# Expert biases by a GpSimd row broadcast and VectorE adds instead of bias matmuls

## The chip, the cores and the metric

The kernel runs on one core of one Trainium2 chip. The metric is the device time of one execution in microseconds (us). The kernel before takes 2105.02 us, the median of 3 runs (2104.12 to 2105.26). A core has five engines with a queue each: TensorE (PE; PEld is its weight load), VectorE (DVE), ScalarE (ACT), GpSimd (POOL) and SyncE (SP, which here only issues DMAs). Each engine takes its instructions strictly in the order of its queue.

## The reference

One layer of a bidirectional encoder on 1024 tokens of width 1024: a hybrid mixer, cross attention to 256 memory tokens, and a mixture of experts with 32 experts of which each token takes 4. Only the last concerns us. For a block of rows `xb` of expert `e`:

```
gu   = xb @ w_gate_up[e] + b_gate_up[e]
gate = minimum(gu[:, :1024], 7);  up = clip(gu[:, 1024:], -7, 7)
glu  = gate * sigmoid(1.702 * gate)
out  = ((up + 1) * glu) @ w_down[e] + b_down[e]
```

Each `out` row is added, with its router weight, to its token's row of the result. The two bias halves of `b_gate_up[e]`, 1024 gate and 1024 up values, lie along the columns of `gu`, and each of them is the same for all rows of the block.

## The kernel before

The stages up to the router take the first 620 us or so. Then the 32 experts follow one another. Each has up to 128 rows in the main path (`main_mm`, `glu_main`, `h_main`, `y_main`: tokens on the partitions of the result) and some have 32 or 64 rows beyond these, which go by a path of their own (`rem_mm`, `h_rem`, `y_rem`); experts with such rows are called heavy, the others light, and heavy and light ones alternate for the most part.

An expert's weights are 12 chunks of 1 MB (128 partitions x 2048), loaded by SP (`load_more`, L964). Chunks 0 to 7 are gate and up, four for each half `c` of the 1024 hidden columns; chunks 8 to 11 are the down projection. Most chunks are split into a leading part and a rest (`split`, L132: ACT writes `eh`, DVE subtracts and writes `el`), and multiplied in three products, L1062 to L1064. The first 8 chunks of the first expert and the last 4 of the last are multiplied whole, L1054.

The order of all queues is written out by hand. `expert` (L1147) goes chunk by chunk; an expert has 24 places, two for each chunk, and at place p what is listed for it is issued: `glu_main` for half 0 at place 7 and for half 1 at place 15; the transposes of the hidden values (`h_main`) of half 0 at place 11 or 13 and of half 1 at 16 to 18; the transposes of the next expert's gathered rows (`x_main`, from the tile `xg`) at places 20 to 23; `y_main` (L1127), which scales the results on ACT and adds them to the tokens by a scatter DMA of POOL, after place 23. Splits run some chunks ahead of the products, by the tables `AHEAD_*`. The dictionary `agenda` holds what is put at places counted over all experts, 24 for each.

POOL has, for each expert, the gathers of the next expert's rows (L936: `xg`, and `xgr` where there are rows beyond), and the scatters L940 of `yr` and `y`. POOL also issues the first expert's later chunks.

The biases are added by matmuls: the table `BT` holds the gate biases of all experts on 64 partitions (leading parts and rests) and the up biases on the other 64, and for each expert and half two matmuls, L1049, with a one-hot column `ohr` as weights write the bias row to all rows of the banks `g` and `u` before the first product. `bias_load` and `bias_table` (L1228, L1234) make the table. `glu` (L998) then has four DVE instructions on 128 x 512: clamp of gate out of PSUM (L1000), clamp of up out of PSUM (L1002), gate times sigmoid (L1003), and (up + 1) times that (L1004), with the sigmoid on ACT (L1001). The tile tag `s4` has 7 buffers; `BT` holds one of them to the end.

Of the kernel before, what the change touches and what calls it, by code (L numbers as in the profile page):

```python
# [29 lines left out]
ALPHA = 1.702  # L30
N64 = 2
# [18 lines left out]
REM = (2, 4, 0, 4, 4, 1)  # L50
PLACE_HEAVY = (13, 17, 19, 21)
# [28 lines left out]
def kernel(ctx: ExitStack, tc: tile.TileContext, A, out, dbg=None):  # L80
# [39 lines left out]
    def rsqrt(dst, v, tmp):  # L120
        """1 / sqrt of positive columns times RS: a first guess from the exponent, three Newton steps, each without its last factor"""
# [29 lines left out]
    def sum_cols(srcs):  # L151
        """sums over the partitions, a token on each partition, 128 tokens for each column; among the products that follow"""
        b = sm_bank("colps")
        k = 0
        for src in srcs:
            for j in range(src.shape[-1] // P):
                def one(k=k, s=src[:, j * P:(j + 1) * P]):
                    nc.tensor.matmul(b[:, k:k + 1], s, ones[:, 0:1], start=True, stop=True)
                fill.append(one)
                k += 1  # L160
        return b[:, :k]

    def rms_cols(b, width, eps_scale=1.0):
        """sums of squares to 1 / rms"""
# [20 lines left out]
    def rms_row(dg, dst):  # L185
        """on every partition, a token in each column"""
# [20 lines left out]
    # weights in their order of use: raw ahead, split one ahead  # L207
# [44 lines left out]
    # ---------------------------------------------------------------- constants  # L252
# [34 lines left out]
    # ------------------------------------------------------------ x^T and the Fourier group's projection  # L287
# [75 lines left out]
    # Fourier group: fold over n <-> N - n and n <-> N/2 - n, channel transform  # L363
# [45 lines left out]
    # short convolution group  # L409
# [98 lines left out]
    # ------------------------------------------------------------ sequence transform, memory side  # L508
# [14 lines left out]
    def seq_out(ct, sb):  # L523
        """in three parts"""
# [82 lines left out]
    # ------------------------------------------------------------ output projection and first residual  # L607
# [41 lines left out]
    # ------------------------------------------------------------ attention over the memory  # L649
    # scale of the logits: rms / sqrt(head dim), one column for each token tile  # L650
# [88 lines left out]
    # v W_o for each head, then the second residual  # L739
# [20 lines left out]
    def row_table():  # L760
        """table of expert rows, all padding"""
# [17 lines left out]
    def load_bias():  # L779
        """leading parts twice, then the rests: products with leading part, rest, leading part of the weights"""  # L780
# [14 lines left out]
    # ------------------------------------------------------------ router, one tile of 128 tokens at a time  # L795
# [3 lines left out]
    BT = []  # L799

    def tile_r(x2):
        """logits of two tiles, an expert on each partition, in four parts"""
# [113 lines left out]
    # ------------------------------------------------------------ experts  # L916
# [60 lines left out]
    def whole(q):  # L977
        """chunks that are multiplied in float32 itself, where the tensor engine has the time"""
# [59 lines left out]
    def main_mm(i, j, middle=None):  # L1038
# [3 lines left out]
        if g == 0 and j >= 8:  # L1042
            s[key] = mm_bank(key)
        elif g == 0 and t == 0:
            r = s["r"]
            for t in range(2):
                tsl = slice(t * 64, t * 64 + 64)
                b = s["gu"[t] + str(c)] = mm_bank(key)
                nc.tensor.matmul(b, ohr[tsl, r:r + 1].to_broadcast([64, P]), BT[0][tsl, hs[c]], start=True, stop=False)  # L1049
        raw, wh, wl = ch[12 * i + j][:3]  # L1050
        ps = s[key]
        if wh is None:
            for k in range(4):
                nc.tensor.matmul(ps, f(l[:, 0, g * 4 + k, :]), raw[:, k, :], start=j >= 8 and g == 0 and k == 0, stop=g == 1 and k == 3)  # L1054
# [5 lines left out]
        for k in range(4):  # L1060
            kk = g * 4 + k
            nc.tensor.matmul(ps, l[:, 0, kk, :], wh[:, k, :], start=j >= 8 and g == 0 and k == 0, stop=False)  # L1062
# [7 lines left out]
    def rem_mm(i, j):  # L1070
        """rows 128.. of the pair of chunks j - 1, j: products for different rows of PSUM run side by side"""
# [18 lines left out]
    def glu_main(i, c):  # L1090
        s = st[i]
        s[f"h{c}"] = t2("hh")
        glu(s[f"h{c}"], s[f"g{c}"], s[f"u{c}"], H2, P)
# [11 lines left out]
    def h_rem(i, c):  # L1105
        """hidden values with the columns on the partitions; each sum has two parts"""
# [40 lines left out]
    def expert(i, hook=None, last=False):  # L1147
        """a chunk at a time; what else there is to do has its place after the first half of a chunk or after the chunk"""
# [50 lines left out]
    def plan(i):  # L1199
        """rows 128.. of an expert: some chunks ahead of the first 128, so that raw chunks are not held for them"""  # L1200
# [12 lines left out]
    for i in range(1, NE):  # L1213
        if rem_rows(order[i]):
            plan(i)

    # ------------------------------------------------------------ second residual, chunk by chunk
    def early():
        """positions of the static expert: rows of the first tiles within its first 128, the others beyond"""
# [7 lines left out]

    def bias_load():  # L1228
        """gate biases on the first half of the partitions, up biases on the second: a leading part and the rest of each expert"""
        BT.extend([s4("BT", [P, D], F32R), s8("braw", [P, D])])  # L1230
        for i in range(4):
            nc.scalar.dma_start(out=BT[1][i * 32:(i + 1) * 32], in_=A["b_gate_up"][:, (i // 2) * D:(i // 2 + 1) * D])

    def bias_table():  # L1234
        nc.scalar.activation(BT[0], BT[1], AF.Copy)
        for i in (32, 96):
# [369 lines left out]
```

## Time and profile before

| | |
|---|---|
| time, median of 3 | 2105.02 us (2104.12 to 2105.26) |
| span of the profiled execution | 2097.7 us |
| PE busy | 2059.9 us (98%) |
| DVE busy | 1590.7 us (76%) |
| ACT busy | 1124.9 us (54%) |
| POOL busy | 233.0 us (11%) |
| DMA moved | 514.06 MB, 245 GB/s over the span |

The span runs from the first to the last instruction of the profiled execution; the device time of a run is some 7 us longer. In a row of the timeline the first number is the start in us from the span's start, the second the busy time, then engine, line, operation, output <- input, and in brackets the idle time ahead of it with what ended it. The rows that the prediction uses stand in a section of their own below.

### The profile page before, as it was taken

Reading aid. Unit: us, or ns where it says so; the run is one execution under the profiler, and the core shown is the slowest. Engines: PE = TensorE matmul, PEld = TensorE weight load, DVE = VectorE, ACT = ScalarE, POOL = GpSimd, SP = SyncE. Lnnn points to the kernel's source line nnn. Section 1 sums busy time; section 2 is a strip of 40 time slices with the busy share of each in tenths; the row PEclk is TensorE's granted clock in tenths of the full one; section 3 lists DMA queues with packets and bytes.
Section 4 is the critical chain, followed back from the end, with each engine's and each line's share of the span. In section 5 each row is a group of like instructions: output and inputs, shape, how many; then the busy total and the mean of one; then the engine's idle time right before and its main releaser. Section 6 shows DMA issues by size and latency. Waiting matters only on the chain. (4 is left out here: it accounts for less than half of the span.)

```text
span 2097.7 us, 28863 instructions
## 1 busy us (share of the span) xinstructions
PE 2059.9 (98%) x10857; PEld 1521.2 (73%) x10857; DVE 1590.7 (76%) x2000; ACT 1124.9 (54%) x1200; POOL 233.0 (11%) x192
## 2 busy tenths in 40 slices
PE   8999999999989999999999999999999999999996
PEld 7888988888974567676777676767667767676764
DVE  6666778445666667888888897888888888888886
ACT  5233533344223455676566665667656567566764
POOL 0000100000232111011101011102111101110101
PEclk9999999999999999999999999999999999999998
DMA  4121434013266769897989887988798989798986
GB/s 156 50 65 61 146 120 157 21 41 124 94 245 252 249 224 327 296 327 267 340 309 366 300 318 272 343 304 325 278 331 313 356 296 320 273 344 306 341 303 241
DMA packets 105327, 514.06 MB, mean 245 GB/s; under 512 B 21697, under 2 KB 26050, under 8 KB 56034
## 3 DMA queue, kind: packets, MB, share of 16 engines
q1 hardware_dynamic: 83968, 445.88, 56.3%
q0 software_dynamic: 14400, 49.33, 9.6%
q10 hardware_dynamic: 6818, 16.99, 2.2%
q8 instruction: 86, 1.41, 0.3%
q14 instruction: 55, 0.45, 0.1%
HBM read 473.81 MB, written 38.34 MB: 244 GB/s over the span
## 5 line engine op out<-in xcount | busy, mean ns | idle before, releaser
L135 DVE TENSOR_TENSOR el<-raw,eh 128x2048 fp32r<-128x2048 f32 x372 | 831.3, 2287 | 134.6 <-ACT eh L134 133.1
L134 ACT ACTIVATE eh<-raw 128x2048 fp32r<-128x2048 f32 x372 | 690.5, 1908 | 7.2 <-PEq L1402 4.6
L1062 PE MATMUL g<-eh,xthl 128*128 128x512 f32 x992 | 401.3, 405 | 0.0
L1063 PE MATMUL g<-el,xthl 128*128 128x512 f32 x992 | 388.5, 392 | 2.0 <-DVE el L135 2.0
L1064 PE MATMUL g<-eh,xthl 128*128 128x512 f32 x992 | 388.2, 391 | 2.2 <-issue 2.2
L1062 PEld LDWEIGHTS g<-eh,xthl 128*128 128x128 f32 x992 | 186.5, 188 | 80.8 <-issue 42.6
L1064 PEld LDWEIGHTS g<-eh,xthl 128*128 128x128 f32 x992 | 186.6, 188 | 43.5 <-issue 2.6
L1063 PEld LDWEIGHTS g<-el,xthl 128*128 128x128 f32 x992 | 186.8, 188 | 37.9 <-DVE el L135 2.7
L1062 PE MATMUL d<-eh,hthl 128*128 128x512 f32 x496 | 205.9, 415 | 0.0
L1064 PE MATMUL d<-eh,hthl 128*128 128x512 f32 x496 | 195.0, 393 | 0.0
L1063 PE MATMUL d<-el,hthl 128*128 128x512 f32 x496 | 193.9, 391 | 0.0
L1085 PE MATMUL r<-raw,xrt 128*32 128x512 f32 (+1 forms) x1216 | 166.3, 598 | 0.7 <-ACT xrt L1036 0.7
L1001 ACT ACTIVATE sg<-g 128x512 f32<-128x512 f32 x64 | 40.4, 631 | 171.1 <-DVE g L1000 171.1
L940 POOL DMA_INDIRECT acc_d<-y,idx x31 | 78.2, 2522 | 384.7 <-ACT y L1131 302.4
L1062 PEld LDWEIGHTS d<-eh,hthl 128*128 128x128 f32 x496 | 93.2, 188 | 27.2 <-ACT xthl L134 9.2
L1064 PEld LDWEIGHTS d<-eh,hthl 128*128 128x128 f32 x496 | 93.1, 188 | 21.2
L1063 PEld LDWEIGHTS d<-el,hthl 128*128 128x128 f32 x496 | 93.6, 189 | 16.0
L1085 PEld LDWEIGHTS r<-raw,xrt 128*32 128x32 f32 (+1 forms) x1216 | 39.8, 113 | 87.0 <-issue 85.8
L134 ACT ACTIVATE hthl<-tp 128x512 fp32r<-128x512 f32 x62 | 37.1, 599 | 119.4 <-PE tp L1009 119.4
L145 PE MATMUL mm<-xh,wh 128*128 128x512 f32 x232 | 92.4, 398 | 5.8 <-ACT xh L137 5.8
L147 PE MATMUL mm<-xh,wl 128*128 128x512 f32 x232 | 91.2, 393 | 0.3 <-DVE wl L135 0.3
L146 PE MATMUL mm<-xl,wh 128*128 128x512 f32 x232 | 91.2, 393 | 0.0
(377 smaller groups left out, 3297.7 us busy)
## 6 DMA issues: line engine op xcount, KB each, us to landing
raw<-in_w_exp SPq DMA_DIRECT2D x375, 1024.0 KB
raw<-in_w_exp POOLq DMA_DIRECT2D x9, 1024.0 KB
wraw<-in_w_in SPq DMA_DIRECT2D x15, 512.0 KB
xraw<-in_xT SPq DMA_DIRECT2D x16, 256.0 KB
wraw<-in_w_k SPq DMA_DIRECT2D x8, 512.0 KB
wraw<-in_w_v SPq DMA_DIRECT2D x8, 512.0 KB
wraw<-in_w_out SPq DMA_DIRECT2D x8, 512.0 KB
xres<-in_xT SPq DMA_DIRECT2D x16, 256.0 KB
```

Of the source, the lines that this page charges most:

```text
L134: nc.scalar.activation(dh, src, AF.Copy)
L135: nc.vector.tensor_tensor(dl, src, f(dh), op=ALU.subtract)
L145: nc.tensor.matmul(ps, lh, rh, start=start and i == 0, stop=False)
L146: nc.tensor.matmul(ps, lh, rl, start=False, stop=False)
L147: nc.tensor.matmul(ps, ll, rh, start=False, stop=stop and i == n - 1)
L940: nc.gpsimd.indirect_dma_start(out=dst, out_offset=bass.IndirectOffsetOnAxis(ap=idx, axis=0), in_=src, in_offset=None, compute_op=ALU.add)
L1001: nc.scalar.activation(sg[:m, :n], g[:m, :n], AF.Sigmoid, scale=ALPHA)
L1062: nc.tensor.matmul(ps, l[:, 0, kk, :], wh[:, k, :], start=j >= 8 and g == 0 and k == 0, stop=False)
L1063: nc.tensor.matmul(ps, l[:, 0, kk, :], wl[:, k, :], start=False, stop=False)
L1064: nc.tensor.matmul(ps, l[:, 1, kk, :], wh[:, k, :], start=False, stop=g == 1 and k == 3)
L1085: nc.tensor.matmul(ps[o:o + m], lhs[:, g * 4 + kk, :], ch[12 * i + j - 1 + t][0][:, kk, :], start=k == 0 and g == 0, stop=k == 4 // n - 1 ...
```

## The change

The bias matmuls, their table and the one-hot column go. For each expert `i` and half `c`, `bias_row` loads the 512 gate and 512 up biases into partition 0 of a tile `bt` (tag `s4`, 128 x 2 x 512) by an SP DMA, and `bias_rows` has POOL add 1 to the up biases and copy partition 0 to all partitions. `BIAS` gives the places: for half 0 the load at place -3 (three places ahead of the expert's start) and the copy at place 1; for half 1 at places 5 and 9. `glu_main` adds the biases out of PSUM and takes the clamps along: 5 DVE instructions. Rows beyond 128 keep `h_rem` as it was. The comments and docstrings that the changed file leaves out are not shown.

```
+SIGMOID_LIMIT = float(1.0 / (1.0 + np.exp(-ALPHA * LIMIT)))
+BIAS = ((-3, 1), (5, 9))
...
 def main_mm(i, j, middle=None):
-        if g == 0 and j >= 8:
+        if g == 0:
             s[key] = mm_bank(key)
-        elif g == 0 and t == 0:
-            r = s["r"]
-            for t in range(2):
-                tsl = slice(t * 64, t * 64 + 64)
-                b = s["gu"[t] + str(c)] = mm_bank(key)
-                nc.tensor.matmul(b, ohr[tsl, r:r + 1].to_broadcast([64, P]), BT[0][tsl, hs[c]], start=True, stop=False)
...
 def glu_main(i, c):
-        glu(s[f"h{c}"], s[f"g{c}"], s[f"u{c}"], H2, P)
+        g, sg, u = t2("g"), t2("sg"), t2("u")
+        bt = s[f"b{c}"]
+        nc.vector.tensor_tensor(g, s[f"g{c}"], bt[:, 0, :], op=ALU.add)
+        nc.scalar.activation(sg, g, AF.Sigmoid, scale=ALPHA)
+        nc.vector.tensor_tensor(u, s[f"u{c}"], bt[:, 1, :], op=ALU.add)
+        nc.vector.tensor_scalar(u, u, LIMIT + 1.0, 1.0 - LIMIT, op0=ALU.min, op1=ALU.max)
+        nc.vector.scalar_tensor_tensor(u, sg, SIGMOID_LIMIT, u, op0=ALU.min, op1=ALU.mult)
+        nc.vector.scalar_tensor_tensor(s[f"h{c}"], g, LIMIT, u, op0=ALU.min, op1=ALU.mult)
+
+    def bias_row(i, c):
+        s = st[i]
+        bt = s[f"b{c}"] = s4("bt", [P, 2, H2])
+        nc.sync.dma_start(out=bt[0:1], in_=A["b_gate_up"][ds(s["e"], 1)].rearrange("o (t c f) -> o t c f", t=2, c=2)[:, :, c, :])
+
+    def bias_rows(i, c):
+        bt = st[i][f"b{c}"]
+        nc.gpsimd.tensor_scalar(bt[0:1, 1, :], bt[0:1, 1, :], 1.0, None, op0=ALU.add)
+        nc.gpsimd.partition_broadcast(bt.rearrange("p t f -> p (t f)"), bt[0:1].rearrange("p t f -> p (t f)"))
...
-    for i in range(1, NE):
-        if rem_rows(order[i]):
+    for i in range(NE):
+        for c, (row, rows) in enumerate(BIAS):
+            if i or c:
+                agenda.setdefault(24 * i + row, []).append(lambda i=i, c=c: bias_row(i, c))
+            agenda.setdefault(24 * i + max(rows, 0 if i else 1), []).append(lambda i=i, c=c: bias_rows(i, c))
+        if i and rem_rows(order[i]):
             plan(i)
...
-    def bias_load():
-        BT.extend([s4("BT", [P, D], F32R), s8("braw", [P, D])])
-        for i in range(4):
-            nc.scalar.dma_start(out=BT[1][i * 32:(i + 1) * 32], in_=A["b_gate_up"][:, (i // 2) * D:(i // 2 + 1) * D])
-    def bias_table():
-        nc.scalar.activation(BT[0], BT[1], AF.Copy)
-        for i in (32, 96):
-            nc.vector.tensor_tensor(BT[0][i:i + 32], BT[1][i:i + 32], f(BT[0][i:i + 32]), op=ALU.subtract)
...
-    nc.vector.tensor_copy(ohr[:, STATIC:STATIC + 1], eid[:, 4:5])
+    bias_row(0, 0)
     x_main(0, 0)
     tile_r(xD)
-    bias_table()
     x_main(0, 1)
...
-            nc.vector.tensor_copy(ohr, R)
```

POOL's queue over two experts in the middle of the program, from the scatter of one expert's results (`acc_d<-y`) to that of the one after the next, before:

```order
L940 DMA acc_d<-y,idx 1152x1024
L936 DMA xg<-h_d,idx 128x1024
L936 DMA xgr<-h_d,idr 32x1024
L940 DMA acc_d<-y,idx 1152x1024
L936 DMA xg<-h_d,idx 128x1024
L940 DMA acc_d<-yr,ids 2304x512
L940 DMA acc_d<-y,idx 1152x1024
```

And the first of these two experts now, on the same queue, with the two copies of biases into `bt`, for half 0 and half 1; an ISA row without operands names, in the built program, the library of GpSimd code that the next instruction needs (index 0 ahead of the tensor_scalar, index 1 ahead of the broadcast, which is the ISA row with operands):

```order
L941 DMA acc_d<-y,idx 1152x1024
L1106 ISA
L1106 TENSOR_SCALAR bt<-bt 1x512
L1107 ISA
L1107 ISA bt<-bt 128x1024
L937 DMA xg<-h_d,idx 128x1024
L937 DMA xgr<-h_d,idr 32x1024
L1106 ISA
L1106 TENSOR_SCALAR bt<-bt 1x512
L1107 ISA
L1107 ISA bt<-bt 128x1024
L941 DMA acc_d<-y,idx 1152x1024
```

Between two scatters stand eight more rows, four of which ask for another library, and the gathers of the next expert's rows now stand behind four of them or behind all eight.

VectorE at the end of a half of a heavy expert, `g` and `u` being the PSUM banks with the products, `hh` the hidden values, before:

```order
L135 TENSOR_TENSOR el<-raw,eh 128x2048 x6
L1000 TENSOR_SCALAR g<-g_8469 128x512
L1002 TENSOR_SCALAR u<-g_8471 128x512
L1003 TENSOR_TENSOR g<-g,sg 128x512
L1004 SCALAR_TENSOR_TENSOR hh<-u,g 128x512
L1116 TENSOR_TENSOR re<-tp,bT 128x256
```

The same place now:

```order
L137 TENSOR_TENSOR el<-raw,eh 128x2048 x6
L1090 TENSOR_TENSOR g<-g_8501,bt 128x512
L1092 TENSOR_TENSOR u<-u_8516,bt 128x512
L1093 TENSOR_SCALAR u<-u 128x512
L1094 SCALAR_TENSOR_TENSOR u<-sg,u 128x512
L1095 SCALAR_TENSOR_TENSOR hh<-g,u 128x512
L1130 TENSOR_TENSOR re<-tp,bT 128x256
```

One instruction is added, and the first of the five now reads `bt`, which POOL writes.

TensorE where one expert ends (`d`) and the next begins (`g`), before:

```order
L1064 MATMUL d_7946<-eh,hthl 128x512
L1085 MATMUL r_8034<-raw,xrt 32x512 x8
L1049 MATMUL g_8051<-BT,ohr 128x512
L1049 MATMUL g_8053<-BT,ohr 128x512
L1062 MATMUL g_8051<-eh,xthl 128x512
```

The two rows L1049 are gone from the queue at this place, and at the one in the middle of each expert; nothing else moves on TensorE.

## Rows read from the trace of the kernel before

**Rows 1.** The page's first part: engine, busy us (share), instructions.

```profile
PE 2059.9 (98%) x10857; PEld 1521.2 (73%) x10857; DVE 1590.7 (76%) x2000; ACT 1124.9 (54%) x1200; POOL 233.0 (11%) x192
```

**Rows 2.** Busy us of each engine in a stretch of experts, granted clock, DMA share, GB/s.

```profile
1200.00:1400.00 200.00, 200.00 (x1037) 141.65 (x1036) 168.30 (x149) 131.16 (x110) 26.67 (x16) 1.00 0.85 309
```

**Rows 3.** Timeline of TensorE at the start of an expert.

```profile
1043.96 0.39 PE L1063 MATMUL g<-el,xthl 128*128 128x512 f32 x1
1044.19 0.39 PE L1064 MATMUL g<-eh,xthl 128*128 128x512 f32 x1
1044.51 0.50 PE L1049 MATMUL g<-BT,ohr 64*128 64x512 f32 x2
1044.94 0.50 PE L1062 MATMUL g<-eh,xthl 128*128 128x512 f32 x1
1045.28 0.39 PE L1063 MATMUL g<-el,xthl 128*128 128x512 f32 x1
```

**Rows 4.** Groups of VectorE instructions and L1049: count, busy us, mean ns, idle before.

```profile
L1049 PE MATMUL g<-BT,ohr 64*128 64x512 f32 x128 | 32.3, 501 | 0.0
L1002 DVE TENSOR_SCALAR u<-g 128x512 f32<-128x512 f32 x64 | 44.0, 687 | 18.1 <-PE g L1064 14.3 <-PE g L1054 2.7
L1004 DVE SCALAR_TENSOR_TENSOR hh<-u,g 128x512 f32<-128x512 f32 x64 | 44.3, 692 | 2.2
L628 DVE TENSOR_TENSOR mm<-mm,row 128x512 f32<-128x512 f32 x32 | 22.3, 698 | 15.2 <-PE mm L147 15.0
L696 DVE TENSOR_SCALAR pr<-pr,st 128x256 f32<-128x256 f32 x32 | 9.9, 351 | 0.6
```

**Rows 5.** Timeline of POOL at the program's start.

```profile
0.35 0.12 POOL L1596 MEMSET const-uint8-127<- 128x1 uint8 x1
0.87 0.15 POOL L277 IOTA ioti<- 128x32 int32 x1 [0.40 <-POOLq L1596]
```

**Rows 6.** Timeline of POOL in a heavy and a light expert.

```profile
1030.96 1.45 POOL L940 DMA_INDIRECT acc_d<-yr,ids  x1 [20.16 <-ACT yr L1142]
1039.31 1.98 POOL L940 DMA_INDIRECT acc_d<-y,idx  x1 [6.89 <-DMA acc_d<-yr,ids]
1046.17 1.16 POOL L936 DMA_INDIRECT xg<-h_d,idx  x1 [4.88 <-DMA idx<-tab_d]
1047.63 0.89 POOL L936 DMA_INDIRECT xgr<-h_d,idr  x1 [0.30 <-issue]
1070.88 2.39 POOL L940 DMA_INDIRECT acc_d<-y,idx  x1 [22.37 <-ACT y L1131]
```

**Rows 7.** Timeline of SP's queue: the load of the rows' indices for that gather.

```profile
1040.13 0.34 SPq L946 DMA_DIRECT2D idx<-tab_d  x1
```

**Rows 8.** POOL by groups, and L940: ns min/median/max, first and last start us.

```profile
L198 POOL TENSOR_TENSOR row<-row,sq 128x512 f32<-128x512 f32 x6 | 10.1, 1704 | 249.2 <-ACT sq L197 249.2
L763 POOL IOTA ptab<- 128x288 int32 x1 | 0.4, 387 | 216.8 <-DVE vtl L135 216.8
L1493 POOL TENSOR_TENSOR fa<-fa,gfin 128x1024 f32<-128x1024 f32 x2 | 4.7, 2365 | 17.9 <-ACT fa L1492 17.9
L940 POOL DMA_INDIRECT acc_d<-y,idx x31: 1579/2390/3519, 700.0 to 2050.3; - x31
L940 POOL DMA_INDIRECT acc_d<-yr,ids x19 | 28.2, 1484 | 474.7 <-ACT yr L1142 377.9 <-ACT yr L1144 96.8
```

**Rows 9.** Timeline of DVE and PE around the second half's hidden values, heavy then light.

```profile
1015.32 0.68 DVE L1000 TENSOR_SCALAR g<-g 128x512 f32<-128x512 f32 x1
1017.50 0.69 DVE L1004 SCALAR_TENSOR_TENSOR hh<-u,g 128x512 f32<-128x512 f32 x1
1021.18 0.60 PE L1009 MATMUL tp<-cst,hh 128*128 128x128 f32 x4
...
1055.19 0.68 DVE L1000 TENSOR_SCALAR g<-g 128x512 f32<-128x512 f32 x1
1057.97 0.69 DVE L1004 SCALAR_TENSOR_TENSOR hh<-u,g 128x512 f32<-128x512 f32 x1
1060.53 0.60 PE L1009 MATMUL tp<-cst,hh 128*128 128x128 f32 x4
```

More of the change, by code (lines that the diff above doesn't have):

```diff
@@ L798 @@
     lt = {}
-    BT = []
     def tile_r(x2):
@@ L1053, in main_mm @@
             for k in range(4):
-                nc.tensor.matmul(ps, f(l[:, 0, g * 4 + k, :]), raw[:, k, :], start=j >= 8 and g == 0 and k == 0, stop=g == 1 and k == 3)
+                nc.tensor.matmul(ps, f(l[:, 0, g * 4 + k, :]), raw[:, k, :], start=g == 0 and k == 0, stop=g == 1 and k == 3)
                 if k % 2 and steps:
@@ L1061, in main_mm @@
             kk = g * 4 + k
-            nc.tensor.matmul(ps, l[:, 0, kk, :], wh[:, k, :], start=j >= 8 and g == 0 and k == 0, stop=False)
+            nc.tensor.matmul(ps, l[:, 0, kk, :], wh[:, k, :], start=g == 0 and k == 0, stop=False)
             nc.tensor.matmul(ps, l[:, 0, kk, :], wl[:, k, :], start=False, stop=False)
@@ L1273 @@
     xB = x2_chunk(HF, places(*two_tiles(0, xA, 0)))
-    C = two_tiles(2, xB, HF)
-    C[5].append((bias_load,))
-    xC = x2_chunk(H2, places(*C))
+    xC = x2_chunk(H2, places(*two_tiles(2, xB, HF)))
     prologue(0)
@@ L1289 @@
     dump("acc", acc_d)
-    ohr = small("ohr", [P, NE], F32R)
     ordr = small("ordr", [1, NE + 1], I32)
-    nc.vector.tensor_copy(ohr[:, STATIC:STATIC + 1], eid[:, 4:5])
+    bias_row(0, 0)
     x_main(0, 0)
     tile_r(xD)
-    bias_table()
     x_main(0, 1)
```

## The prediction

> **What bounds the kernel now.** I read the page's first part, then the busy times by stretch, then the timelines of the engines that the change touches. TensorE is busy for 98% of the span [rows 1], and in a stretch of experts for all of its 200 us, at a granted clock of 1.00 [rows 2]. So what is taken off TensorE there comes off the time, as long as nothing else becomes later than TensorE. VectorE is the next, with 168.3 of 200 us; POOL has 26.7 of 200 and mostly waits: in the timeline its scatter of `y` waits 22.37 us for ScalarE's `y` [rows 6]. POOL is nearly idle, but it stands on a loop through every expert: the gather of the next expert's rows comes behind the scatter of the last one's results, and now the biases come between.
>
> The period of that loop is read from the scatters of `y`: 31 of them, the first at 700.0 us, the last at 2050.3, so 30 periods of 45.0 us on the mean [rows 8].
>
> **What the change removes.** Each pair of bias matmuls costs more on TensorE's path than the busy time tells, since it breaks the rhythm of the products. Products start 0.23 us apart (1043.96 to 1044.19); across the pair the starts are 1044.19 and 1044.94, and the next 0.34 later [rows 3]. That is 0.75 - 0.23 + 0.34 - 0.23 = 0.63 us for each of the 64 pairs (128 matmuls, 32.3 us busy [rows 4]), 40 us in all. This is the gain if TensorE stays the bound. Making the table once, ahead of the first expert, goes too; I put that at nothing (a microsecond or two of ScalarE and VectorE in a stretch that waits for the router anyway).
>
> **What it adds on VectorE.** Four instructions become five, 64 times. Adds out of PSUM with a second input from SBUF have a row, 698 ns on the same shape; scalar_tensor_tensor has 692 [rows 4]. The clamp of `u` is from SBUF to SBUF, between 351 ns (half the width) and 687 [rows 4]; I take 0.6. So the five take 4 x 0.69 + 0.6 = 3.4 us. VectorE gains up to 64 x 0.69 = 44 us of work; in 200 us with 4.4 experts that is 8.8 x 0.69 = 6 us, 174 of 200. Not a bound. Late hidden values don't follow either: from the end of `hh` to its transposes are 3.0 us in the heavy and 1.9 us in the light expert [rows 9], more than 0.69.
>
> **What it adds on POOL.** For each half expert: a request for library 0, a tensor_scalar on 512 elements, a request for library 1, a broadcast of 1024. The two computing instructions have near rows. A two-input add of 512 elements takes 1.70 us, I take that for the tensor_scalar; an iota of 288 takes 0.387, which is 1.4 for 1024, and a two-input product of 1024 takes 2.37 [rows 8]; between them I take 1.8 for the broadcast.
>
> The price of a change of library decides this case, and the trace before shows no change of library, only one request, for the library that is already there at the program's start: from the last memset at 0.35 to the iota at 0.87 pass 0.52 us, 0.40 of them idle [rows 5]. That is the bound below. [...] The loading of one kilobyte of indices is issued at 1040.13 and its gather starts at 1046.17: 6.0 us [rows 6, 7]. And a DMA of POOL's own, the scatter of `yr` that starts at 1030.96, holds up the next scatter until 1039.31: 8.35 us [rows 6]. [...]
>
> [...]
>
> **The sum.** A half costs POOL 7.2 + 1.7 + 7.2 + 1.8 = 17.9 us, two halves 35.8, and they stand in the loop one after the other. The loop, from one scatter of `y` to the next: the scatter 2.4 (median [rows 8]); the biases of half 0, then of half 1, 35.8; the gathers that stand between or behind, 1.0 for `xg` and 0.9 for `xgr` in about 18 of 30 experts [rows 6, 8], 1.6 on the mean; VectorE's five instructions of half 1, 3.4; then the tail, from the transposes of half 1's hidden values over the last chunks and the scaling of `y` to the scatter: 1021.18 to 1039.31, 18.1 us, in the heavy expert, 1060.53 to 1070.88, 10.4 us, in the light one [rows 6, 9], with 18 heavy of 30 (19 scatters of `yr`, one of them the first expert's) 15.0. Together 2.4 + 35.8 + 1.6 + 3.4 + 15.0 = 58.2 us, against 45.0 now: TensorE no longer sets the period, and its 40 us are not gained but sit in waits. 30 x 13.2 = 396 us more. The profiled span of 2097.7 becomes about 2494, and with the 7.3 us that lie between that span and the median of 2105.02, the time is 2501, say **2500 us**.
>
> What is queued behind the waiting instructions: on VectorE, behind the add that waits for `bt`, the splits of the next chunks, and TensorE waits for these. By the tables they run some 3 to 5 chunks ahead, and a chunk lasts 45.0 / 12 = 3.75 us, so they cover 11 to 19 us of a wait once, but not one in each half expert. On POOL, behind the library requests, the gather `xg`, whose transposes stand on TensorE at places 20 to 23. On SP, the load of a `bt` row waits until a buffer of tag `s4` is free, among others until POOL has done an earlier copy, and the 1 MB chunks are queued behind it; with POOL late this comes late too, but inside the same loop. In the first expert three of its chunks and one gather stand behind a copy on POOL; that happens once, 0 to 20 us, and I leave it out of the middle value.
>
> **The rivals.**
> *Changing the library is cheap* (up to about 2 us, near the row of 0.52). Then a half is at most 2 x 2 + 3.5 = 7.5 us, the loop 15 + 22.4 = 37 us, TensorE keeps the bound, and the 40 us are gained: 2065 us. For it: the one request in the trace cost next to nothing. Against it: that one changed nothing. This is the case on the other side. Chance 0.10.
> *It breaks even*: 3 to 4 us for each change give a loop of 2.4 + 19 to 23 + 20.0 = 41 to 45 us, about the period now. 2065 to 2120 us. Chance 0.05, 0.03 of it within 0.2% of the time before (about what a measurement of this kernel can tell from no change), 0.02 slower.
> [...] From about 11 us for a change on the time is above my range. Chance 0.10.
> *VectorE becomes the bound* with its fifth instruction: by the row of 168.3 of 200 us it doesn't, and the time would then only lose part of the 40 us. Chance under 0.02, within the first rival's.
>
> **How the numbers follow.** 0.75 for the forecast, that a change of library costs between 4.5 and 11 us. Each microsecond of it is worth 4 x 30 = 120 us. 4.5 us gives a loop of 47.4 us and 2177; 11 us gives 73.4 and 2957. So the range is 2180 to 2960, which leaves out the cheap and the breaking-even cases below and the two-trip case above. Faster 0.10, same 0.03, slower 0.87.
>
> **What would show it.** The scatters of `y` should lie about 58 us apart instead of 45. POOL's timeline should show, from a tensor_scalar to its broadcast, a gap of 6 to 9 us that no engine's row explains, and the same gap ahead of the tensor_scalar. VectorE should wait for POOL at the add of `g`, about 64 times, several us each; TensorE's busy share should fall to about 82% (2020 of 2494), with its waits put down to the splits, the hidden values and `xg`. If the gap is under 2 us and TensorE stays at 98 to 100% among the experts, the price of the library was wrong and the time is near 2065. If the gaps are right and the period is not, the tail was wrong: TensorE may have done in the wait what I count behind it, as the heavy expert's tail has work for other rows in it.

## The result, and the profile after

The changed kernel takes 2666.89 us (median of 4 runs, 2658.85 to 2677.37) against 2104.57 us for the kernel before in the same comparison: a ratio of 1.2677, 95% interval 1.2642 to 1.2713. That is slower, as forecast, inside the range, and 167 us above the predicted 2500. In the following `bt` is the tile of biases, a *copy* is GpSimd's `partition_broadcast` of its first row, and a *change* is the time that GpSimd loses when it goes from one library to the other. Of the lines of the kernel after, L941 and L937 are L940 and L936 of before, L137 is L135, L1010 is L1009, and L1057 to L1059 are L1062 to L1064; `hthl` are the split, transposed hidden values, which the down products take as weights.

The page's first part, after (columns as in [rows 1]):

```profile
PE 2166.5 (81%) x10729; PEld 1594.7 (60%) x10729; DVE 1623.0 (61%) x2060; ACT 1115.6 (42%) x1199; POOL 434.9 (16%) x320
```

And the stretch from 1200 to 1400 us (columns as in [rows 2]):

```profile
1200.00:1400.00 200.00, 152.61 (x718) 106.94 (x719) 126.94 (x117) 92.24 (x78) 35.76 (x22) 0.85 0.59 211
```

No engine is near full in this stretch any more: TensorE has gone from 200.00 to 152.61 us, VectorE from 168.30 to 126.94, and POOL, the only one that has grown, is at 35.76. Nothing is slower because an engine has too much work; something waits. POOL's groups show where:

```profile
L1106 POOL TENSOR_SCALAR bt<-bt 1x512 f32<-1x512 f32 x64 | 128.4, 2006 | 566.2 <-issue 449.4 <-PE g L1059 70.8 <-DVE el L137 46.0
L1107 POOL PARTITION_BROADCAST bt<-bt x64 | 85.1, 1329 | 444.7 <-issue 391.4 <-DMA raw<-in_w_exp 37.9 <-DMA bt<-in_b_gate_up 9.5
```

The two instructions cost 213.5 us of work and 1010.9 us of idle time ahead of them, most of it put down to "issue", that is, to nothing that the profile shows: 7.9 us for each of 128. The scatters of `y` (ns min/median/max, first and last start):

```profile
L941 POOL DMA_INDIRECT acc_d<-y,idx x31: 1566/2535/3667, 716.4 to 2592.0; - x31
```

The 30 periods went from 45.0 to (2592.0 - 716.4) / 30 = 62.5 us. The first scatter is 16.4 us later than in [rows 8], and from the last one to the end of the span it is 71.8 instead of 47.4. Together 16.4 + 525 + 24.4 = 566, the difference of the spans (2663.8 and 2097.7). The loop holds 93% of the loss. Light experts lose most of it: from scatter to scatter they take 58.7 us on the mean instead of 31.7, the heavy ones 65.1 instead of 53.9 (12 and 18 periods, so 324 and 202 us).

POOL's timeline after, from a heavy expert's scatter over the whole next, light one:

```profile
1288.59 2.18 POOL L941 DMA_INDIRECT acc_d<-y,idx  x1 [7.28 <-DMA acc_d<-yr,ids]
1300.71 1.52 POOL L1106 TENSOR_SCALAR bt<-bt 1x512 f32<-1x512 f32 x1 [9.95 <-issue]
1309.28 1.30 POOL L1107 PARTITION_BROADCAST bt<-bt  x1 [7.05 <-DMA raw<-in_w_exp]
1310.78 1.19 POOL L937 DMA_INDIRECT xg<-h_d,idx  x1 [0.20 <-issue]
1312.27 0.88 POOL L937 DMA_INDIRECT xgr<-h_d,idr  x1 [0.30 <-issue]
1320.30 1.52 POOL L1106 TENSOR_SCALAR bt<-bt 1x512 f32<-1x512 f32 x1 [7.15 <-issue]
1327.71 1.30 POOL L1107 PARTITION_BROADCAST bt<-bt  x1 [5.89 <-issue]
1346.89 2.53 POOL L941 DMA_INDIRECT acc_d<-y,idx  x1 [17.87 <-ACT y L1145]
```

Four gaps of 6 to 10 us stand between short instructions, and then POOL, which has just made everybody wait, waits itself for the result of the expert that it delayed. That is the loop. (One gap is put down to a chunk's DMA: it was only the last to finish in that time.) What VectorE waits for most in the whole span (us in total, times, longest):

```profile
DVE g L1090 <- POOL bt L1107: 571.6, 62, 18.3
```

And TensorE:

```profile
PE tp L1010 <- DVE hh L1095: 349.0, 45, 18.9
PE d L1059 <- DVE hthl L137: 44.8, 17, 2.9
```

TensorE loses more than its waits. Its timeline behind one of them:

```profile
1332.47 1.09 PE L1010 MATMUL tp<-cst,hh 128*128 128x128 f32 x4 [9.33 <-DVE hh L1095]
1334.63 0.63 PE L1057 MATMUL d<-eh,hthl 128*128 128x512 f32 x1
1335.06 0.63 PE L1058 MATMUL d<-el,hthl 128*128 128x512 f32 x1
...
1344.45 0.39 PE L1058 MATMUL d<-el,hthl 128*128 128x512 f32 x1
1344.67 0.39 PE L1059 MATMUL d<-eh,hthl 128*128 128x512 f32 x1
```

Busy times and granted clock in the two pieces of it:

```profile
1332.40:1340.00 7.60, 7.53 (x26) 5.78 (x27) 6.71 (x4) 4.47 (x4) 0.00 (x0) 0.50 0.54 206
1341.50:1345.40 3.90, 3.90 (x21) 3.17 (x19) 1.39 (x2) 2.38 (x4) 0.00 (x0) 1.00 0.00 0
```

After standing for 9.33 us its products start 0.43 us apart at a granted clock of 0.50, and 0.22 us apart when the clock is back at 1.00. The same 10729 instructions are 2036.7 us of busy time in the first experiment below, which hardly waits, and 2166.5 here.

### The profile page after: what moved, and what is told of

Read it like the earlier page. It is cut to its first block, busy times and chain, and to the rows that moved or that the text cites. A ratio compares the mean times of both kernels' runs of the same rounds, so it can differ in the third digit from the quotient of the medians.

```text
span 2663.8 us, 29516 instructions
## 1 busy us (share of the span) xinstructions
PE 2166.5 (81%) x10729; PEld 1594.7 (60%) x10729; DVE 1623.0 (61%) x2060; ACT 1115.6 (42%) x1199; POOL 434.9 (16%) x320
## 3 DMA queue, kind: packets, MB, share of 16 engines
q1 hardware_dynamic: 84224, 446.15, 44.6%
## 5 line engine op out<-in xcount | busy, mean ns | idle before, releaser
L137 DVE TENSOR_TENSOR el<-raw,eh 128x2048 fp32r<-128x2048 f32 x372 | 840.7, 2313 | 145.5 <-ACT eh L136 145.5
L1090 DVE TENSOR_TENSOR g<-g,bt 128x512 f32<-128x512 f32 x64 | 44.3, 692 | 571.6 <-POOL bt L1107 571.6
L1010 PE MATMUL tp<-cst,hh 128*128 128x128 f32 x256 | 56.9, 364 | 355.9 <-DVE hh L1095 349.0
L1010 PEld LDWEIGHTS tp<-cst,hh 128*128 128x128 f32 x256 | 38.7, 185 | 380.0 <-issue 369.1
L1059 PE MATMUL d<-eh,hthl 128*128 128x512 f32 x496 | 222.1, 448 | 45.0 <-DVE hthl L137 44.8
L1057 PE MATMUL d<-eh,hthl 128*128 128x512 f32 x496 | 233.6, 471 | 24.6 <-ACT hthl L136 24.6
L1106 POOL TENSOR_SCALAR bt<-bt 1x512 f32<-1x512 f32 x64 | 128.4, 2006 | 566.2 <-issue 449.4
L1057 PE MATMUL u<-eh,xthl 128*128 128x512 f32 x496 | 210.9, 425 | 9.4 <-POOL bt L1106 9.4
L1058 PE MATMUL u<-el,xthl 128*128 128x512 f32 x496 | 206.0, 415 | 0.2 <-DVE el L137 0.2
L1059 PE MATMUL u<-eh,xthl 128*128 128x512 f32 x496 | 204.5, 412 | 0.0
L1057 PE MATMUL g<-eh,xthl 128*128 128x512 f32 x496 | 202.9, 409 | 0.2 <-issue 0.2
L1058 PE MATMUL g<-el,xthl 128*128 128x512 f32 x496 | 195.9, 395 | 0.6 <-DVE el L137 0.6
L1059 PE MATMUL g<-eh,xthl 128*128 128x512 f32 x496 | 194.5, 392 | 0.5 <-DVE xthl L137 0.5
L1107 POOL PARTITION_BROADCAST bt<-bt x64 | 85.1, 1329 | 444.7 <-issue 391.4
L1059 PEld LDWEIGHTS d<-eh,hthl 128*128 128x128 f32 x496 | 108.7, 219 | 80.9 <-DVE hthl L137 54.9
L1057 PEld LDWEIGHTS d<-eh,hthl 128*128 128x128 f32 x496 | 109.5, 221 | 58.9 <-ACT hthl L136 28.4
L941 POOL DMA_INDIRECT acc_d<-y,idx x31 | 79.9, 2578 | 323.9 <-ACT y L1145 248.0
L1057 PEld LDWEIGHTS g<-eh,xthl 128*128 128x128 f32 x496 | 93.6, 189 | 63.7 <-issue 43.8
```

Of the source, the lines that this page charges most:

```text
L137: nc.vector.tensor_tensor(dl, src, f(dh), op=ALU.subtract)
L941: nc.gpsimd.indirect_dma_start(out=dst, out_offset=bass.IndirectOffsetOnAxis(ap=idx, axis=0), in_=src, in_offset=None, compute_op=ALU.add)
L1010: nc.tensor.transpose(tb[:, j * P:(j + 1) * P], src(j), ident)
L1057: nc.tensor.matmul(ps, l[:, 0, kk, :], wh[:, k, :], start=g == 0 and k == 0, stop=False)
L1058: nc.tensor.matmul(ps, l[:, 0, kk, :], wl[:, k, :], start=False, stop=False)
L1059: nc.tensor.matmul(ps, l[:, 1, kk, :], wh[:, k, :], start=False, stop=g == 1 and k == 3)
```

## The experiments

The theory: a change costs 7 to 10 us, four of them stand in a loop through each expert, and the loop has become longer than TensorE's work. Rivals: the tensor_scalar is what is slow, not the change; VectorE's wait at the add is the price and an earlier copy would hide it; the fallen clock is a price of its own; VectorE's fifth instruction takes part. e2, e3, e4, x3 and y3 were run once each. Each run is compared with the kernel before that ran beside it, whose median lay between 2098.35 and 2100.3 us.

### e1: no tensor_scalar on POOL

```diff
-        nc.vector.tensor_tensor(u, s[f"u{c}"], bt[:, 1, :], op=ALU.add)
+        nc.vector.scalar_tensor_tensor(u, s[f"u{c}"], 1.0, bt[:, 1, :], op0=ALU.add, op1=ALU.add)
-        nc.gpsimd.tensor_scalar(bt[0:1, 1, :], bt[0:1, 1, :], 1.0, None, op0=ALU.add)
```

> The 1 is added by VectorE in the instruction that reads the up products out of PSUM (scalar_tensor_tensor in place of tensor_tensor, as many VectorE instructions as in the changed kernel); POOL only copies the row, so that one library stays loaded from expert to expert. Theory (the changes of library are the price): a half costs POOL one broadcast of 1.3 us, TensorE is the bound again among the experts and its 40 us of bias matmuls are gained: 2065 us, up to 2090 if some copies come late. Rival A (the hand-over is the price: VectorE waits for a POOL copy in every half, whatever it consists of): only the part of POOL's own time goes, 2300 us or more. Rival B (VectorE's fifth instruction, or POOL and VectorE getting in each other's way during the copies): little changes, 2550 us or more.

2123.51 us, ratio to before 1.0122 [1.0103, 1.0142]. Of the 562 us, 538 are gone with this one instruction. POOL's group of copies has 18.3 us of "issue" ahead of it instead of 391.4:

```profile
L1106 POOL PARTITION_BROADCAST bt<-bt x64 | 147.5, 2304 | 164.5 <-DMA bt<-in_b_gate_up 123.4 <-issue 18.3 <-DVE el L137 17.4
```

But the kernel is still slower than before, where 2065 to 2090 was expected. A part of it is at the ends. POOL's timeline in the first expert holds those 18.3 us; an iota, which shares the tensor_scalar's library (after, its 0.18 us start at 654.21 and the tensor_scalar follows at 654.39, without a gap), still stands between two copies. It shares no data with them, and both it and the copy behind it have the gap, so the gap is no wait of one instruction for the other's result:

```profile
625.14 1.30 POOL L1106 PARTITION_BROADCAST bt<-bt  x1 [8.84 <-issue]
...
649.01 0.18 POOL L1314 IOTA rk<- 32x64 f32 x1 [7.71 <-DMA idr<-tab_d]
658.62 1.30 POOL L1106 PARTITION_BROADCAST bt<-bt  x1 [9.43 <-issue]
660.13 1.13 POOL L937 DMA_INDIRECT xgr<-h_d,idr  x1 [0.20 <-issue]
```

The first scatter of `y` starts 13.3 us late. At the end the last copy waits 14.58 us for its row, which SP loads behind the loads of `acc_d` for the final stage; the stretch behind the last scatter is 7.2 us longer than before. The rest is in the loop: scatters 44.9 us apart where 45.0 less two pairs at 0.63 gives 43.7. x1 to x4 go into that.

### e2: the tensor_scalar in half 0 alone

```diff
-        nc.gpsimd.tensor_scalar(bt[0:1, 1, :], bt[0:1, 1, :], 1.0, None, op0=ALU.add)
+        if c == 0:
+            nc.gpsimd.tensor_scalar(bt[0:1, 1, :], bt[0:1, 1, :], 1.0, None, op0=ALU.add)
```

(with the add of `u` as in e1 for half 1)

> POOL adds the 1 for half 0 alone, VectorE adds it for half 1: two changes of library for each expert in place of four. Theory (a serial loop through POOL's queue, VectorE and TensorE): half 1's copy comes at once, half 0's is as late as before. From the scatter of y to bt of half 0 stay 2.5 + 9.9 + 1.5 + 7.0 + 1.3 = 22 us, and from place 7 to the next scatter 16 places of 1.8 us = 29 us: a period of about 51 us, (51 - 45) x 30 = 180 us over the kernel before, 2290 us. Rival A (each change costs its share of the loss wherever it stands): half of 562 us goes, 2385 us. Rival B (not the changes of library): 2600 us.

2492.01 us: a miss, 107 us above the nearest of the expected times. Half of the changes cost not half of the loss but 70% of it. The scatters are 56.9 us apart. VectorE's longest wait:

```profile
DVE g L1090 <- POOL bt L1111: 392.7, 31, 18.6
```

It now waits once for an expert, for half 0. The copy of half 0 is done some 23 us behind the scatter, and from there the way to the next scatter is longer than from half 1: everything that TensorE's order puts between half 0 and the end stands behind it (24.4 us in a light expert, against 16.1 from half 1 in the kernel after). The expectation had 29 us for this way in every expert. In a light one that was too much; in a heavy one, where TensorE has the rows beyond 128 to do as well, it is about 40 us, and that is the miss. Two changes were taken out of the loop, and the loop took another, longer way round.

### e3: the changes alone, nobody waits for their data

The kernel before, with a pair of idle instructions on POOL at the places of the copies:

```diff
...
+    def swaps():
+        nc.gpsimd.tensor_scalar(idle[0:1, 1, :], idle[0:1, 1, :], 1.0, None, op0=ALU.add)
+        nc.gpsimd.partition_broadcast(idle.rearrange("p t f -> p (t f)"), idle[0:1].rearrange("p t f -> p (t f)"))
+    for i in range(NE):
+        for p in (1, 9):
+            agenda.setdefault(24 * i + p, []).append(swaps)
```

> The kernel before, with its bias matmuls, and beside them at the same two places of each expert a tensor_scalar and a broadcast of POOL on a scratch tile of 16 columns that nobody reads: the same changes of library without VectorE waiting for a result. Theory: POOL has 4 x 7.9 us of changes and some 6 us of its own work for each expert, less than the period of 45, but the gather of the next rows stands behind two or four changes and comes 0 to 8 us late in some experts: 2150 to 2300 us, with TensorE waiting at the transposes of xg and not at those of hh. Rival A (all of the loss is VectorE's wait for bt): 2105 us. Rival B (the changes themselves disturb DMAs or other engines): 2500 us or more.

2471.62 us, a miss again, between the theory's range and its rival's 2500, and the more telling. POOL's waits ahead of the idle pair:

```profile
POOL idle L1221 <- issue: 612.4, 62, 12.1
POOL idle L1222 <- issue: 355.3, 53, 10.3
```

And what TensorE waits for:

```profile
PE tp L1009 <- DMA xg<-h_d,idx: 169.1, 18, 12.6
PE tp L1035 <- DMA xgr<-h_d,idr: 101.0, 13, 10.0
```

No wait for a bias exists here, the bias matmuls are all there, and 372 us are lost: POOL is late with the next expert's gather and TensorE stands for it. Of the 372 us between the two spans, 301 are more idle time of TensorE, 270 of it in these two waits, and 71 are longer busy time (2130.9 us instead of 2059.9 for the same instructions) at a mean granted clock of 0.926 instead of 0.995. Little is left for a disturbance of other engines or DMAs by the changes. So VectorE's wait is one way in which the loss shows, not its cause. The loop closes through the gather as well.

### e4: loads and copies six places earlier

`BIAS` is shifted by six places for the experts behind the third.

> The changed kernel with both loads and both copies six places earlier from the fourth expert on (half 0 loaded at place -9 and copied at -5, half 1 at -1 and 3): no change of library less. Theory (serial loop): half 0's copy now stands ahead of the scatter of the last results and overlaps with the tail, so the loop has one half's 19 us instead of two: 2.5 + 20 + 1.7 + 3.4 + 15 = 43 us, with POOL's own time of about 45 us for each expert as the bound: 2120 to 2250 us. Rival (POOL's time itself is the price, wherever it stands): 2600 us or more.

2403.08 us, 264 less than after and 153 above the upper end of what the theory expected. POOL's timeline at the end of a light expert:

```profile
892.70 1.66 POOL L1107 PARTITION_BROADCAST bt<-bt  x1 [5.82 <-issue]
894.57 3.46 POOL L941 DMA_INDIRECT acc_d<-y,idx  x1 [0.21 <-ACT eh L136]
```

In the light experts the scatter of `y` now follows the last copy by 0.2 us on the mean, so POOL has no free time left in them (42.3 us from scatter to scatter, where e1 has 31.5). In most of the heavy ones it is the scatter of `yr` that follows as closely. Six places earlier does not hide the changes: with POOL's own work they fill it.

### y3: tensor_scalars alone

e3 with the idle copy replaced by a second tensor_scalar.

```diff
-        nc.gpsimd.partition_broadcast(idle.rearrange("p t f -> p (t f)"), idle[0:1].rearrange("p t f -> p (t f)"))
+        nc.gpsimd.tensor_scalar(idle[:, 0, :], idle[:, 0, :], 1.0, None, op0=ALU.add)
```

> e3 with its 64 idle copies replaced by a second idle tensor_scalar (128x8): 128 tensor_scalars on GpSimd that nobody waits for, and no copy, at the same places of the kernel before. e1 had only the copies, and no gaps ahead of them. If the gap of 7 to 12 us belongs to going from the one kind to the other, it is gone here but for one at the start, and the time is 2100 to 2125 us; if each tensor_scalar brings it by itself, whatever stood before it, GpSimd loses at least the 612 us that e3's showed, and the time is 2450 us or more.

2102.74 us beside 2100.3 for before, whose runs go from 2096.3 to 2101.9: nothing to speak of. POOL's groups:

```profile
L1222 POOL TENSOR_SCALAR idle<-idle 128x8 f32<-128x8 f32 x64 | 104.7, 1636 | 0.0
L1221 POOL TENSOR_SCALAR idle<-idle 1x8 f32<-1x8 f32 x64 | 94.6, 1478 | 0.3
```

128 tensor_scalars with 0.3 us of idle time ahead of them. Copies alone (e1) lose nothing to "issue" in the loop either. Only both together have them, in e3 and after. The price belongs to the change from one kind to the other; that is shown. What GpSimd does in that time is not: the profile has no transfer for it (the two instruction queues of the page hold 147 packets after and 141 before, for 128 changes).

### x3: TensorE kept at work in the wait

The kernel after with 16 extra products ahead of each group of `h` transposes.

```diff
...
+        for j in range(warm):
+            nc.tensor.matmul(tb[:, :2 * P], ident, cst, start=True, stop=True)
...
```

> The changed kernel, with 16 extra fp32 products of 128x256 (their results are overwritten) ahead of each group of h transposes of experts 1 to 30. They fill part of the time in which TensorE stands for h. If the lower clock (0.893 in the mean, 2166.5 us busy against some 2037 us for the same instructions at 0.99) is a price of its own behind each wait, the warm clock gives some of those 130 us back: up to 60 us less than 2667 us. If the wait alone is the price, or the extra products don't hold the clock: the same 2667 us, or up to 30 us more, since they take some of TensorE's time themselves.

2715.97 us, the rival's side, 19 us beyond its 30. The page's first part:

```profile
PE 2496.2 (92%) x12649; PEld 1908.5 (70%) x12649; DVE 1623.9 (60%) x2060; ACT 1116.3 (41%) x1199; POOL 432.4 (16%) x320
```

The stretch from 1200 to 1400 us:

```profile
1200.00:1400.00 200.00, 189.41 (x934) 142.54 (x935) 128.58 (x119) 91.15 (x78) 37.80 (x23) 0.96 0.59 215
```

And the group of the extra products:

```profile
L1010 PE MATMUL tp<-cst 128*128 128x256 f32 x1920 | 426.1, 380 | 0.0
```

The clock is up from 0.85 to 0.96, and the kernel's own instructions take 2496.2 - 426.1 = 2070 us instead of 2166. In the light experts the way from the last copy to the scatter is shorter for it, 14.3 us on the mean instead of 16.1; in the heavy ones the extra products don't fit into the wait and it is longer, 27.9 instead of 22.7. So the lower clock costs a light expert's tail about 2 us, by this one run, and 92% of busy TensorE can be a kernel that is 2% slower.

### x1, x2, x4: what the bias matmuls are worth

x1 is the kernel before without the pairs of bias matmuls, so that these biases are left out of the computation:

```diff
-        if g == 0 and j >= 8:
+        if g == 0:
...
-                nc.tensor.matmul(b, ohr[tsl, r:r + 1].to_broadcast([64, P]), BT[0][tsl, hs[c]], start=True, stop=False)
...
```

> The kernel before without its 64 pairs of bias matmuls; nothing is put in their place, so the biases of gate and up are left out (the table that holds them is still made). It prices the pair alone, with GpSimd and VectorE as before. Theory A, the prediction's term: TensorE is the bound, a pair is 0.63 us on its path, 64 of them 40 us: 2059 us. Rival: the pair is worth less, because VectorE or a DMA becomes the later one in part of the time; e1 went from 45.0 to 44.9 us between y scatters instead of 43.7, and if that is the true price of the pair, this run stays above 2085 us.

2071.84 us, ratio 0.9872 [0.985, 0.9895]: 26.5 us, or 0.41 for a pair, between the two expectations. TensorE's busy time falls by 33.8 us (2059.9 to 2026.1), not by 40, and 7.8 of them come back as idle time (37.8 to 45.6 us of the spans). 26 us, not 40, is what taking the pairs away is worth with nothing put in their place.

x2 is e1 with both ends mended:

```diff
...
+        nc.gpsimd.partition_broadcast(pre, pre[0:1])
...
-        for c, (row, rows) in enumerate(BIAS):
+        for c, (row, rows) in enumerate(((-3, 1), (-2, 4)) if i == NE - 1 else BIAS):
...
-        nc.gpsimd.iota(iob, pattern=[[1, NBLK]], base=0, channel_multiplier=0, allow_small_or_imprecise_dtypes=True)
+        nc.vector.tensor_copy(iob[:, :NE], iot[:NE])
+        nc.vector.tensor_scalar(iob[:, NE:], iot[:NE], float(NE), None, op0=ALU.add)
```

> e1 (GpSimd only copies, the +1 in VectorE's add) with the two ends mended: the copy's library is loaded by a copy of 8 columns at the start, while GpSimd waits for the routing; the second iota is made by VectorE, so that no change back is needed; the last expert's second bias row is loaded two places before the expert starts. Theory: e1 lost 13.3 us at the first y scatter and 7.2 us behind the last, so 2123.5 - 13 - 7 = 2103 us, the same as before within 0.3%; the middle stays at 44.9 us from y scatter to y scatter. Rival: the late start was hidden later, because TensorE's order absorbs it: then above 2115 us.

2096.70 us, ratio 0.9991 [0.9978, 1.0005]: level with before. The first scatter is back at 700.1 us. The loop is as in e1, 45.0 us, so the 26 us are still lost in it. Busy times from the first scatter of `y` to the last in x1:

```profile
695.40:2025.80 1330.40, 1320.69 (x6824) 936.13 (x6823) 1116.36 (x984) 849.92 (x725) 165.67 (x95) 0.99 0.86 315
```

and in x2:

```profile
700.10:2051.70 1351.60, 1324.76 (x6820) 929.15 (x6819) 1187.35 (x1044) 846.48 (x725) 285.85 (x156) 1.00 0.85 310
```

With the same products TensorE is idle for 27 us in x2 and for 10 in x1, and VectorE has 71 us more to do. What TensorE waits for in x2 there:

```profile
PE d L1062 <- DVE hthl L137: 11.4, 11, 1.5
PE tp L1013 <- DVE hh L1098: 8.5, 13, 0.7
```

x4 is e1 without the clamp of `u` (which is left out of the computation), so that VectorE has four instructions for a half:

```diff
-        nc.vector.tensor_scalar(u, u, LIMIT + 1.0, 1.0 - LIMIT, op0=ALU.min, op1=ALU.max)
```

> e1 without VectorE's clamp of up (the instruction of 0.46 us; that clamp is left out of the computation). VectorE then has four instructions for a half instead of five, as many as before the change. If VectorE's longer chain for each half is what took half of the gain of the bias matmuls, the y scatters come 43.5 to 44.2 us apart instead of 44.9 and the time is 2080 to 2105 us. If it is GpSimd's and VectorE's slowing of one another, or a DMA: within 8 us of e1's 2123 us.

2105.46 us, ratio 1.0029 [1.0015, 1.0043], from e1's 1.0122: about 18 us for 0.46 us less a half. That is just outside what the theory expected, at most 2105 us and 44.2 us between scatters, which are 44.6 apart. The two profiles show 8 us of it, from the first scatter to the last; the rest is not located, since the profiled executions (2114.28 and 2116.53 us) are only 2 us apart where the medians are 18. VectorE's work takes part of the gain; y1 goes into that.

### y1, y4, y5: versions that beat both kernels by 1%

The splits of the weights into a leading part and a rest, VectorE's largest group, show the rest of it. Groups of x2:

```profile
L137 DVE TENSOR_TENSOR el<-raw,eh 128x2048 fp32r<-128x2048 f32 x372 | 875.8, 2408 | 118.2 <-ACT eh L136 118.2
L1109 POOL PARTITION_BROADCAST bt<-bt x64 | 142.7, 2230 | 129.1 <-DMA bt<-in_b_gate_up 110.6 <-ACT re L1119 12.1 <-DVE u L1095 5.6
```

and of y4 below, where the DMA does the copying:

```profile
L137 DVE TENSOR_TENSOR el<-raw,eh 128x2048 fp32r<-128x2048 f32 x372 | 831.1, 2287 | 130.9 <-ACT eh L136 129.5
```

With POOL's copies beside it a split takes 2408 ns, without them 2287, as before; and a copy takes 2230 ns instead of the 1329 that it took after, when VectorE mostly stood waiting for it. The two slow one another; in what way, no run here shows.

y1 is x2 with the sigmoid replaced by one function of ScalarE that gives g * sigmoid(1.702 g) (632 ns on 128 x 512, where the sigmoid took 631), here and for the rows beyond 128:

```diff
-        nc.scalar.activation(sg, g, AF.Sigmoid, scale=ALPHA)
+        nc.scalar.activation(sg, g, AF.Gelu_apprx_sigmoid)
...
-        nc.vector.scalar_tensor_tensor(u, sg, SIGMOID_LIMIT, u, op0=ALU.min, op1=ALU.mult)
-        nc.vector.scalar_tensor_tensor(s[f"h{c}"], g, LIMIT, u, op0=ALU.min, op1=ALU.mult)
+        nc.vector.scalar_tensor_tensor(s[f"h{c}"], sg, GLU_LIMIT, u, op0=ALU.min, op1=ALU.mult)
...
```

> x2 with one VectorE instruction less for each half: ScalarE computes g * sigmoid(1.702 g) in one function instead of the sigmoid, and VectorE clamps that product where it multiplies it with up (the clamp of gate and the product with the sigmoid go). VectorE has four instructions for a half and 44 us less work in all. Theory (VectorE's work and the slowing by GpSimd's copies took the gain of the bias matmuls): x4 gave 18 us for 0.46 us less a half, so this gives 18 to 27 us on x2's 2097: 2070 to 2079 us, faster than both kernels. Rival (the clamp of up counted only because it made the chain ahead of the h transposes longer, and that is already hidden in x2): 2085 us or more.

2077.80 us, ratio 0.9895 [0.988, 0.9909], inside the theory's 2070 to 2079.

y4 is x2 with the row read 128 times by the load, and no copy:

```diff
-        nc.sync.dma_start(out=bt[0:1], in_=A["b_gate_up"][ds(s["e"], 1)].rearrange("o (t c f) -> o t c f", t=2, c=2)[:, :, c, :])
+        nc.sync.dma_start(out=bt, in_=A["b_gate_up"][ds(s["e"], 1)].rearrange("o (t c f) -> o t c f", t=2, c=2)[:, :, c, :].to_broadcast([P, 2, H2]))
...
```

> x2 with the rows copied to all partitions by the DMA that loads them (128 times 4 KB, 0.5 MB a half) and no GpSimd copy at all. VectorE's five instructions stay. If GpSimd's copies slow VectorE (el 2408 ns against 2287 before; 120 ns x 372 = 45 us), el falls back to 2.29 us and the time to 2072 to 2085 us. Rival: the 33.5 MB more are the price, since the DMA engines are busy at 0.86 of the middle and rise to 0.93; raw weights come later and the time is 2100 to 2150 us.

2077.59 us, ratio 0.9893 [0.9879, 0.9907], inside the theory's 2072 to 2085. The DMA engines go to 0.92 of the middle, as the rival had it, but TensorE stands for 12 us between the first scatter and the last, no more than in y1 (11).

y5 is both.

> y1 and y4 together: rows copied by the DMA, four VectorE instructions. With neither the copies nor the fifth and fourth product on VectorE it has less work than before the change. If VectorE was all that stood in the way, x1's 2072 us or a little less, 2060 to 2072 us; if the DMA is the price, as much over it as y4 is over 2075 us.

2079.55 us, ratio 0.9919 [0.9902, 0.9935]: no gain on either alone, above the 2060 to 2072 expected. Between the first scatter and the last TensorE is busy for 1317 to 1321 us in x1, y1, y4 and y5 alike, and the scatters are 44.3 to 44.4 us apart in all four. Once VectorE is quick enough, what it saves further is worth nothing here; 10 to 12 us of TensorE's idle time are left, one wait of 6 us and small ones for gathers and splits among them. Of the 8 us by which y5's median is above x1's, the spans of the two profiles show 1.8; the rest lies between executions (y5's go from 2075.6 to 2087.8 us).

## Why the prediction was right, point by point

*The bound and the mechanism* were right: TensorE stopped being the bound, and a loop over POOL took its place. Gaps ahead of both POOL instructions, the 62 waits of VectorE at the add of `g` and the period in the scatters came as the last part of the prediction listed them. e1 and y3 show that it is the change and neither instruction; e3, that it is enough for the loss without any wait of VectorE for a bias.

*Its size*, term by term, the mean of the 30 periods in POOL's timeline (18 heavy, 12 light):

| term of the loop | predicted, us | measured, us |
|---|---|---|
| scatter of `y` | 2.4 | 2.6 |
| four changes | 28.8 | 32.1 |
| two tensor_scalars, two copies | 7.0 | 6.7 |
| gathers between | 1.6 | 1.0 |
| from the last copy to the scatter | 18.4 | 20.0 |
| period | 58.2 | 62.5 |

The step that was too small is *the price of the change*, 7.2 us. It was an estimate, (6.0 + 8.35) / 2 from the two rows [rows 6, 7] in which POOL stands behind a DMA; no run shows that a change is such a wait, so none shows the term. What the kernel after showed in its place is 7.0 us from the tensor_scalar to the copy (64 times, 5.8 to 9.9), 8.3 or 7.2 from a copy or a gather to the tensor_scalar, and 10.4 behind a scatter (31 times, 8.6 to 11.8), 8.0 on the mean of the four in each period. The two rows bracket the mean, but not the gaps behind a scatter; that the place matters was not foreseen. That they came so near is in part luck.

*The tail* was 1.6 us short: 16.1 us in a light expert (13.8 predicted), 22.7 in a heavy one (21.5). In a heavy expert the gathers stand behind the last copy, beside the tail, so that only the light ones' count in the loop (1.0 instead of 1.6). The rows of before show the tail on a TensorE that never stood; behind the wait shown above it runs at half the clock for some 8 us. x3 put that at 1.8 us in a light expert. The same thing is behind a number that came out right for the wrong reason: a busy share of 82% was predicted (its own 2020 of 2494 is 81%) and is 81%, but from 2166 us of busy time and not 2020, in a longer span.

*The once-only costs* were left out of the middle value as 0 to 20 us. They are 16.4 at the start and 24.4 at the end, of which the end was not thought of: behind the last scatter stand all four changes of the last expert, with gaps of 8.7, 9.5, 8.3 and 5.9 us. With 30 x 4.3 = 129 us from the period these 41 us make up the 170 us between the predicted span (2494) and the measured one (2664). The 7.3 us that the prediction adds for the time are not what a run has beyond its span: that is 2 to 3 us in every run on record (2665.65 against 2663.8 here), and the rest lies between executions of the kernel before.

*The gain foregone* was mis-sized: a pair is worth 0.41 us net (x1), not 0.63: 0.53 of TensorE's busy time, of which 0.12 turn into idle time. It changed nothing for a kernel that another loop bounds. *VectorE is no bound* was right for this kernel, and wrong for the rival that ends on the other side: had the change been cheap, the time would have been not 2065 but near e1's 2123, or x2's 2097 with the ends mended. At 179 of 200 us VectorE delays `hh` and `hthl` by fractions of a microsecond that TensorE pays.

*The rivals*: the cheap change and the even one fell with the first gap in POOL's timeline; what lay above the range, a change of 11 us or more, fell with the mean of 8.0, and only single gaps, the longest 11.8 us, come to it. The even one was priced wrongly. The break-even at 3 to 4 us compares a mean loop with a mean period, but heavy and light experts differ. Without its changes the measured loop is 26.7 us in a light expert and 32.9 in a heavy one, against 31.7 and 53.9 of TensorE's own. By these numbers, an estimate, a light expert loses as soon as a change costs more than 1.2 us, and a heavy one only from 5.3; at 3.5 us the twelve light ones would already cost 108 us.

## What to carry to other kernels

Look at which library each GpSimd instruction needs, not only at how long it runs: two cheap ones from different libraries cost 8 us for each change between them here, where either kind alone costs its own 1.3 to 2.3 us. Where steps of two kinds alternate, compare the loop with each kind's own time, not with the mean. An engine that is 11% busy can become the bound if it stands on a loop through every step; price what is put there as latency, and ask which way round the loop goes when one part of it is taken out (e2, e3). And a saving on the bounding engine is worth only what the next engine lets through: here one VectorE instruction less for each half expert decided between no gain (x2) and a gain of 1.1% (y1).

## What was not expected of the hardware

- A change of library took 5.8 to 12 us in the kernel after, the longer ones behind a scatter (10.4 on the mean, against 7.0 behind a tensor_scalar). Why it is longer there stays open. It is not the scatter alone: in e3 the change behind a gather took 10.9 us (12 times), where the kernel after has 7.2.
- A copy of one row to 128 partitions (1024 numbers) takes 1.30 us while VectorE stands and 2.2 beside its splits, which go from 2287 to 2408 ns.
- A DMA that reads a 4 KB row 128 times, 33.5 MB in all, cost no time that shows, with the DMA engines busy at 0.92 (y4's 2077.59 us against 2077.80 for y1, whose rows POOL copies).
- VectorE's clamp from SBUF to SBUF took 427 ns for 128 x 512, where the same clamp out of PSUM took 687 [rows 4].
